# First two modulations as column-group products on TensorE in a two-layer hybrid decoder trunk: input asked for first, rotary tables spread late, planner numbers set anew

## Chip, cores and metric

The kernel runs on one core of one Trainium2 chip. The metric is the device time of one execution in microseconds (us), taken as the median over runs. A core has a matrix engine (TensorE, PE in the profile; PEld is its weight loading), VectorE (DVE), ScalarE (ACT), GpSimd (POOL) and SyncE (SP), which here only issues DMA transfers. Each engine works through its own queue in order.

## The reference

Everything is float32, with one sequence of 1024 rows of width 1024. Layer 0 mixes tokens by sparse attention (an indexer scores all keys, the 256 best are kept per query), layer 1 by a short gated convolution; each is followed by a SwiGLU network of width 2816.

```python
c_act = jax.nn.silu(c)
for i in range(2):
    mod = c_act @ ada_w[i] + ada_b[i]                   # (1, 1024) @ (1024, 6144)
    sh1, sc1, g1, sh2, sc2, g2 = jnp.split(mod, 6, -1)
    h = _rmsnorm(x, norm1_g[i]) * (1.0 + sc1) + sh1
    y = _dsa_mixer(h, ...) if i == 0 else _short_conv_mixer(h, ...)
    x = x + g1 * y
    h = _rmsnorm(x, norm2_g[i]) * (1.0 + sc2) + sh2
    x = x + g2 * _swiglu(h, w_gate[i], w_up[i], w_down[i])
```

Nothing of layer 0 can start before `sc1` and `sh1` of layer 0 (modulations j = 1 and j = 0 of the code) are there: each is a product of a vector of 1024 with a matrix of 1024 x 1024, 4 MB of weights.

## The kernel before

The program is recorded operation by operation (line 246 is the one line that issues them all) and put in order by a planner, class `Plan` (line 162). Every operation has a cost from `Plan.cost` (line 208), a priority `plan.pri` (a planned time in us, smaller first) and its dependencies; `drain` (line 394) plays the engines forward and always issues the operation that can start first, by priority among those that are ready. The numbers `LATENCY`, `SLACK`, `BIAS`, `CHANGE` and `STAY` (lines 164 to 171), the costs, and the planned times of `Attention` (`T_PROJ`, `SLOT`, `t_att`, `until`, lines 814 to 847) thus set the order of the whole program on each engine. The engines then run that order as it stands.

**Start, `first_norm` (line 857).** Eight row tiles of x, 128 x 1024 (512 KB), are loaded and transposed on TensorE; ScalarE squares each for the norm (`junk<-xs`), and ScalarE and VectorE each copy one half of each out of PSUM (`xt<-ps_mm`). `setup` (line 587) loads the small vectors, among them c, and makes `cact` = silu(c) in columns. `rope_tables` (line 727) computes sine and cosine rows, writes them to DRAM (`rd`) and reads them back four times each, spread over partitions into C and S; these ten transfers are issued on ScalarE's queue. The modulations j = 1 and then j = 0 are made from eight loads each of 128 x 1024 (512 KB). Of each load, columns 0 to 639 are multiplied and summed on VectorE (`ada_step`, `sc<-...,cact,sc`), with a sum over partitions on TensorE at the end (`ada_end`, `ps_sm<-ones,sc`); columns 640 to 1023 go through TensorE as three products whose moving operand is one column (`ada_pe`, `ps_mm<-cact,...`), each followed by an add on VectorE (`mod<-ps_mm,mod`). `ada_scale` turns j = 1 into `aff`. Then come, for each half of the 1024 tokens and each of 8 row blocks d, a product with `aff` and the norm on VectorE (`zs` for half 0, `nz` for half 1), the shift rounded to the matmul format on ScalarE (`hhi`) and its remainder on VectorE (`hlo`). x is spilled to DRAM (`xs<-xt`).

**Projections, `project` (line 926).** Each weight block is loaded (`raw`), rounded on ScalarE (`whi`), its remainder taken on VectorE (`wlo`), and used in three products per contraction block (hi hi, hi lo, lo hi). The order is: the index key (72 columns, below called the ki product), the index queries, K, Q in four groups j of 256 columns, V. Between them ScalarE and VectorE bisect for the 256th best score of each query, 31 rounds for each pair of blocks (`select`, line 1151; `junk<-sc,bs`), and `selected` (line 1194) turns the threshold into an additive mask (`bias`). Blocks (2, 3) and (6, 7) are counted on ScalarE, (4, 5) on VectorE; blocks 0 and 1 need no selection.

**Attention, `attend` (line 1217).** For each of 8 query blocks b and 4 key groups g: two paired products of 64 contraction rows (`ps_L<-karena,qst`), mask and maximum on VectorE (`p,mx<-ps_L,bias`), exp on ScalarE, transposes on TensorE (`ident,p`), copies (`pf`), and the products with V, which run as pairs into columns 0 to 63 and 64 to 127 of the array (`values`, line 1304, `ps_o<-pf,vst`, 128 x 64 weights each). `group_end` (line 1331) divides by the sums: reciprocals `rs`, widened by a copy to `rw` (128 x 256), two products of `rw` with the identity, and a multiplication. The gains and the second modulations of layer 0 are made by steps on VectorE in between (`ada_next`, line 1257).

After about 700 us the rest (both feed-forward networks, the convolution) is long chains of 128 x 512 products.

Of the kernel before, what the change touches and what calls it, by code (L numbers as in the profile page):

```python
# [161 lines left out]
class Plan:  # L162
# [3 lines left out]
    SLACK = (0.3, 0.1, 0.1, 0.1, 0.0)  # L166
    WINDOW = 3.41
    LANDING = 2.2
    BIAS = 0.8
    CHANGE = 0.097  # L170
    STAY = 4.0
# [36 lines left out]
    def cost(self, eng, fn, out, ins, kw):  # L208
# [7 lines left out]
        if eng == "tensor":  # L216
            if fn == "transpose":
                return 0.11, 0.0
            if ins[1].dtype in (F32R, BF16):
                return 0.0133 + n / 2400.0, 0.0  # L220
            return 0.112 if n < 64 else n * 4 / 2400.0, 0.0
# [3 lines left out]
        if eng == "scalar":  # L225
            if "accum_out" in kw:
                return 0.17 + 0.845e-3 * n + 0.1 * aps, 0.0
            return 0.04 + 0.83e-3 * n + (0.04 if out.dtype == F32R else 0.0), 0.0
        if eng == "vector":
            if fn == "memset":  # L230
                return 0.02 + 1.04e-3 * (n if n > P else 0), 0.0
            if fn in ("tensor_scalar", "tensor_copy") and not psum and "accum_out" not in kw:
                return (0.08 if fn == "tensor_copy" else 0.13) + 0.52e-3 * m, 0.0
            if fn == "tensor_scalar" and "accum_out" in kw:
                return 0.14 + 1.04e-3 * m, 0.0
            return 0.07 + 1.04e-3 * m + (0.05 * aps if m > 64 else 0.0), 0.0
# [216 lines left out]
P = 128  # L453
# [35 lines left out]
class Trunk:  # L489
# [97 lines left out]
    def setup(self, c, positions, ada_b, n1, n2, conv_w, gq, gk, lg, lb, rope_c, arenas, kgb):  # L587
# [11 lines left out]
        self.plan.pri = 1.2  # L599
# [47 lines left out]
    def ada_end(self, layer, j, lhs, half=0):  # L647
# [8 lines left out]
        dst = self.mod[layer][j]  # L656
        c0 = half * 4
# [3 lines left out]
        if j in (1, 4) and c0 + n == KT or layer == 0 and j == 1:  # L661
# [65 lines left out]
    def rope_tables(self, positions, C, S, tmp, dram):  # L727
# [18 lines left out]
        for i, (out, ph) in enumerate(((C, 0.25), (S, 0.0))):  # L746
# [9 lines left out]
            dr = dram.part_of(i)[i]  # L756
            nc.scalar.dma_start(dr.rearrange("c f t -> (c f) t"), n)
            for rep in range(4):
                nc.scalar.dma_start(
                    out.part_of(rep)[32 * rep:32 * rep + 32, :].rearrange("f (c t) -> f c t",  # L760
                                                                          c=4),
                    dr.rearrange("c f t -> f c t"))
# [50 lines left out]
class Attention:  # L813
    T_PROJ, SLOT = 45.0, 6.2
    ON_ACT, IDX = (2, 3, 6, 7), 0.5

    def __init__(self, tk, w, w_out, ada_w, xspill):
# [26 lines left out]
        cum = np.cumsum([0] + [6.8 * (b + 1) for b in range(TB)])  # L844
        w = np.array([0.0] * 5 + [41.0 / 26 * (c / 6.8 - 10) for c in cum[5:]])
        self.t_att = self.T_PROJ + 38 * self.SLOT + cum + w
        self.until = {2: self.t_att[2], 4: self.t_att[4] + 10.0, 6: self.t_att[7]}
# [9 lines left out]
    def first_norm(self, x, positions, setup):  # L857
# [1115 lines left out]
```

## Time and profile before

| | |
|---|---|
| median of 3 runs | 2283.16 us (2282.76 to 2283.68) |
| the profiled execution | 2284.37 us, of it 2282.7 us span |
| TensorE busy | 2237.3 us, 98% of the span |
| VectorE busy | 1820.4 us, 80% |
| ScalarE busy | 1131.4 us, 50% |
| DMA | 356.37 MB, 156 GB/s on average |

The profile shows one execution; times are counted from the start of the span. A busy TensorE is not one at its peak: the columns of the windows give the clock that was granted (1.00 is 2.4 GHz, 0.50 is 1.2 GHz). A product of float32 operands that are not rounded to the matmul format shows as two records.

### The profile page before, as it was taken

The numbers are of one execution on the slowest core, as the hardware profiler recorded it, in microseconds if no ns is written. First come the engines' busy times: TensorE is split into PE (matmuls) and PEld (weight loads), VectorE is DVE, ScalarE is ACT, GpSimd is POOL, SyncE is SP. The second block draws the span as 40 slices with busy tenths as digits, with TensorE's granted clock in tenths as the row PEclk, the third lists the DMA queues.
The fourth block names the chain that finished last, engine by engine and source line by source line (L and its number), as shares of the span: only waits on it lengthen the run. The fifth ranks groups of instructions, "written<-read, shape, count | busy, mean of one in ns | idle before, by whom it ended". The sixth has DMA issues, their size and how long they took to land.

```text
span 2282.7 us, 33002 instructions
## 1 busy us (share of the span) xinstructions
PE 2237.3 (98%) x11686; PEld 1820.7 (80%) x11686; DVE 1820.4 (80%) x3705; ACT 1131.4 (50%) x2148; POOL 4.1 (0%) x19
## 2 busy tenths in 40 slices
PE   7998999999999999999999999999999999999998
PEld 6666876777798888888888888788888888888887
DVE  5889999776579899987688899885798965667874
ACT  3577899856755333333344553244552333344443
POOL 0000000000000000000000000000000000000000
PEclk6999999999999999999999999999999999999999
DMA  8423233332234566765986154434345633348853
GB/s 273 157 74 84 82 120 91 107 94 66 88 113 138 174 209 203 234 212 183 311 303 213 52 148 134 124 94 165 106 149 175 204 113 99 119 152 308 300 176 97
DMA packets 334191, 356.37 MB, mean 156 GB/s; under 512 B 18089, under 2 KB 218826, under 8 KB 334026
## 3 DMA queue, kind: packets, MB, share of 16 engines
q1 hardware_dynamic: 332586, 352.96, 48.4%
q8 instruction: 91, 1.49, 0.3%
q10 hardware_dynamic: 1440, 1.31, 0.2%
q14 instruction: 74, 0.61, 0.1%
HBM read 282.64 MB, written 71.57 MB: 155 GB/s over the span
## 4 chain that ended last, share of the span: by engine, by line
PE 92%; DVE 4%; ACT 2%; DMA 1%; issue 1%; SPq 0%; ACTq 0%; DVEq 0%
PE ps_x L246 33%; PE ps_mm L246 28%; PE ps_z L246 18%; PE ps_sm L246 6%; PE ps_L L246 4%; PE ps_o L246 3%; ACT junk L246 1%; DVE u L246 0%; DMA raw<-in_conv_w_in_dram 0%; DVE p L246 0%; DMA xs<-in_x_dram 0%; DVE wlo L246 0%; DVE s L246 0%; ACT p L246 0%; DVE sc L246 0%
## 5 line engine op out<-in xcount | busy, mean ns | idle before, releaser
L246 ACT CAST whi<-s 128x512 fp32r<-128x512 f32 x311 | 192.7, 621 | 388.5 <-DVE s L246 116.0
L246 PE MATMUL ps_x<-t,whi 128*128 128x512 f32 x1016 | 314.4, 390 | 0.0
L246 ACT CAST whi<-raw 128x512 fp32r<-128x512 f32 (+1 forms) x228 | 139.5, 618 | 252.4 <-PE ps_z L246 84.4
L246 DVE TENSOR_TENSOR wlo<-s,whi 128x512 fp32r<-128x512 f32 x312 | 213.3, 688 | 47.5 <-ACT whi L246 46.3
L246 DVE TENSOR_TENSOR wlo<-raw,whi 128x512 fp32r<-128x512 f32 (+1 forms) x254 | 173.2, 686 | 75.2 <-ACT whi L246 74.4
L246 PEld LDWEIGHTS ps_x<-t,whi 128*128 128x128 f32 x1016 | 190.8, 188 | 39.6
L246 PE MATMUL ps_x<-t,wlo 128*128 128x512 f32 x508 | 198.1, 390 | 0.0
L246 PE MATMUL ps_x<-h,whi 128*128 128x512 f32 x536 | 165.6, 390 | 0.0
L246 PE MATMUL ps_z<-t,whi 128*128 128x512 f32 x488 | 150.9, 390 | 0.0
L246 DVE CUSTOM_DVE_ANT_0 p<-ps_L,bias 128x512 f32<-128x512 f32 (+3 forms) x192 | 100.3, 553 | 39.8 <-PE ps_L L246 16.7
L246 PE MATMUL ps_z<-h,whi 128*128 128x512 f32 x408 | 126.0, 390 | 0.0
L246 PE MATMUL ps_mm<-h,whi 128*128 128x512 f32 x400 | 123.3, 389 | 0.0
L246 PE MATMUL ps_x<-ph,whi 128*128 128x512 f32 x396 | 122.0, 389 | 0.0
L246 ACT ACTIVATE p<-p,nm,qsc 128x128 f32<-128x128 f32 (+7 forms) x128 | 111.4, 873 | 21.2 <-DVE nm L246 20.0
L246 ACT ACTIVATE junk<-sc,bs 128x896 bf16<-128x896 f32 (+3 forms) x124 | 109.4, 883 | 17.4 <-DVE bs L246 12.5
L246 PEld LDWEIGHTS ps_x<-h,whi 128*128 128x128 f32 x536 | 100.2, 188 | 20.5
L246 PEld LDWEIGHTS ps_x<-t,wlo 128*128 128x128 f32 x508 | 95.5, 188 | 20.2 <-DVE wlo L246 0.2
L246 PEld LDWEIGHTS ps_z<-t,whi 128*128 128x128 f32 x488 | 91.8, 188 | 19.4 <-ACT whi L246 0.3
L246 DVE TENSOR_TENSOR u<-u 128x512 f32<-128x512 f32 x152 | 103.5, 687 | 2.6 <-ACT u L246 0.8
L246 PE MATMUL ps_x<-h,wlo 128*128 128x512 f32 x268 | 104.6, 390 | 0.0
L246 PE MATMUL ps_mm<-hhi,wlo 128*128 128x512 f32 (+2 forms) x240 | 93.0, 389 | 7.3 <-DVE wlo L246 7.2
L246 PE MATMUL ps_z<-t,wlo 128*128 128x512 f32 x244 | 95.6, 392 | 3.9 <-DVE wlo L246 3.9
(379 smaller groups left out, 5406.6 us busy)
## 6 DMA issues: line engine op xcount, KB each, us to landing
adaw<-in_ada_w_dram SPq DMA_DIRECT2D x160, 256.0 KB
ph<-in_ffn_w_down_dram SPq DMA_DIRECT2D x66, 512.0 KB
raw<-in_ffn_w_gate_dram SPq DMA_DIRECT2D x54, 512.0 KB
raw<-in_ffn_w_up_dram SPq DMA_DIRECT2D x54, 512.0 KB
rt<-t SPq DMA_DIRECT2D x80, 256.0 KB
raw<-in_conv_w_in_dram SPq DMA_DIRECT2D x34, 512.0 KB
hid<-u SPq DMA_DIRECT2D x52, 256.0 KB
rt<-hid SPq DMA_DIRECT2D x48, 256.0 KB
```

What stands on the lines that cost most here:

```text
L246: f(*[a.get() if isinstance(a, Ref) else a for a in args], **{k: a.get() if isinstance(a, Ref) else a for k, a in kw.items()})
```

## The change

The first two modulations go to TensorE alone. `cpad` holds, for each of 8 contraction blocks, a 128 x 32 weight whose first column is `cact` and whose others are zero. Each modulation is loaded in two halves of 512 columns, eight loads of 128 x 512 (256 KB) for each half, all into staging tiles with no reuse. Four products of 128 x 32 weights with 128 x 512 float32 operands are issued together, each into its own 32 partitions of one PSUM bank; a second set of four is added on top. ScalarE or VectorE copies the 128 x 512 result, and four products with ones add up the partitions. The shift's modulation is tracked per half, so blocks d = 0 to 3 need only its first half.

```diff
-        bc = [tk.norm_bc(ss.part_of(half)[:, 4 * half:4 * half + 4], sp, "L")[:, 0:HW]
+        bc = [tk.norm_bc(ss.part_of(half)[:, 4 * half:4 * half + 4], sp, "mm")
               for half in range(NH)]
-        plan.pri = 1.5
-        tk.rope_tables(positions, self.C, self.S, self.score[4:2:-1], self.rd)
+        plan.pri = 9.5
+        spread = tk.rope_tables(positions, self.C, self.S, self.score[4:2:-1], self.rd)
+        plan.pri = 1.05
+        cpad = self.score[5][:, 0:32 * KT].rearrange("p (k m) -> p k m", m=32)
+        nc.vector.memset(cpad, 0.0)
+        nc.vector.tensor_copy(cpad[:, :, 0:1], tk.cact.unsqueeze(2))
         for j in (1, 0):
-            acc = self.score[5 + j][:, 0:5 * P]
-            pool, tag = (self.keep, "vst") if j else (self.hp, "lo0")
-            stage = pool.tile([P, 4, D], F32, name="stage%d" % j, tag=tag)
-            for k in range(KT):
-                plan.pri = 10.0 + k + 8 * (1 - j)
...
+            stage = [(self.keep if t == "vst" else self.hp).tile([P, 4, D], F32, name="stage", tag=t)
+                     for t in (("hi1", "vst") if j else ("hi0", "lo0"))]
+            acc, total = tk.ps("L"), self.s4()
+            for half in range(NH):
+                cs = half_of(half)
+                for k in range(KT):
+                    plan.pri = 10.0 + k + 8 * half + 16 * (1 - j)
+                    w = stage[k // 4].part_of((half, k))[:, k % 4, cs]
+                    last = nc.sync.dma_start(w, tk.ada_rows(self.ada_w, 0, j, k)[:, cs])
                 plan.pri = 1.1
-                tk.ada_step(w[:, 0:5 * P], k, acc)
-                tk.ada_pe(w[:, 5 * P:], 0, j, k, 5)
-            tk.ada_end(0, j, [acc])
+                ps = acc.part_of(half)[:, cs]
+                for k0 in (0, 4):
+                    plan.matmuls([(ps[32 * g:32 * g + 32], cpad[:, k0 + g],
+                                   stage[k0 // 4].part_of((half, k0 + g))[:, g, cs])
+                                  for g in range(4)], 1.667e-3, k0 == 0, k0 == 4, base=0.02)
+                row = total.part_of(half)[:, cs]
+                plan.copy(row, ps)
+                tk.ada_end(0, j, [row], half)
+        plan.pri, plan.gate = 42.5, last
+        spread()
+        plan.gate = None
...
-                tk.shift(z, tk.mod[0][0][:, d:d + 1], self.h[half](d))
+                tk.shift(z, tk.mod[0][0].part_of((0, 0, d // 4))[:, d:d + 1], self.h[half](d))
```

The norm's broadcast (`norm_bc`) moves from the PSUM ring `L` to the ring `mm`, which has two buffers and which the ki product uses too. The small loads of `setup` get priority 9.0 in place of 1.2, behind the eight loads of x. The rotary tables' transfers move from ScalarE's queue to SP's: each table is written when its sine is done, and the spreading reads wait for the last modulation load.

```diff
-            nc.scalar.dma_start(dr.rearrange("c f t -> (c f) t"), n)
...
+            nc.sync.dma_start(dram.part_of(i)[i].rearrange("c f t -> (c f) t"), n)
+
+        def spread():
+            for i, out in enumerate((C, S)):
+                for rep in range(4):
+                    nc.sync.dma_start(
...
```

In `group_end` the widening copy goes; four 64-column products take the reciprocals as a broadcast weight:

```diff
-        rw = sp.tile([P, GRP * HD], F32, name="rw", tag="rw")
-        plan.copy(rw.rearrange("p (r d) -> p r d", d=HD),
-                  rs.unsqueeze(2).to_broadcast([P, GRP, HD]))
         bc = self.bank()[:, 0:2 * P]
         for i in range(2):
-            nc.tensor.matmul(bc[:, blk(i)], rw[:, blk(i)], tk.ident, start=True, stop=True)
+            plan.matmuls([(bc[r * HD:(r + 1) * HD, blk(i)],
+                           rs[:, 2 * i + r:2 * i + r + 1].to_broadcast([P, HD]), tk.ident)
+                          for r in range(2)], 1.7e-3)
```

The planner's numbers and costs are set anew, of which two lines stand for all; `until`, which spreads the bisection rounds, ends later for the pairs (2, 3) and (6, 7), and eight modulation steps of attention move from block 2 to block 1.

```diff
-    SLACK = (0.3, 0.1, 0.1, 0.1, 0.0)
+    SLACK = (0.313, 0.045, 0.089, 0.1, 0.0)
...
-        self.until = {2: self.t_att[2], 4: self.t_att[4] + 10.0, 6: self.t_att[7]}
+        self.until = {2: self.t_att[2] + 17.951, 4: self.t_att[4] + 10, 6: self.t_att[7] + 32.655}
```

**What it moves.** SP's queue at the start (`xs` is x, `C`, `S` and `sc` receive the small vectors, `stage`, `raw` and `s` are weights, `rd` the tables in DRAM). Before, one tile of x stands in row 1, and then:

```order
9 L246 DMA S<-in_ada_b_dram 96x128
10 L246 DMA sc_239<-in_positions_dram 32x256 x2
11 L246 DMA S<-in_attn_k_norm_g_dram 1x64
12 L246 DMA sc_239<-in_positions_dram 32x256 x2
13 L246 DMA xs<-in_x_dram 128x1024 x7
14 L246 DMA raw<-in_ada_w_dram 128x1024
15 L246 DMA stage_233<-in_ada_w_dram 128x1024
16 L246 DMA s_247<-in_ada_w_dram 128x1024
```

Now all eight tiles of x stand in row 1, and behind the small vectors:

```order
11 L248 DMA S<-in_attn_k_norm_g_dram 1x64
12 L248 DMA sc_239<-in_positions_dram 32x256 x2
13 L248 DMA stage<-in_ada_w_dram 128x512 x16
14 L248 DMA rd<-sc_240 128x256
15 L248 DMA raw<-in_attn_w_in_dram 128x8x72
16 L248 DMA stage<-in_ada_w_dram 128x512 x12
17 L248 DMA rd<-sc_240 128x256
18 L248 DMA stage<-in_ada_w_dram 128x512 x4
19 L248 DMA raw<-in_attn_w_in_dram 128x4x256 x2
20 L248 DMA C<-rd 32x4x256 x4
21 L248 DMA S<-rd 32x4x256 x4
```

All of x thus stands ahead of the small vectors, the 16 loads of j = 1 follow these in one row, and two writes of tables, each of which waits for a sine on ScalarE, stand between the other modulation loads. Behind row 21 come the 16 spills of x and four weight loads.

TensorE from the modulations to the first product of the ki (`hhi`, `hlo` with `whi`, `wlo`). Before, the last rows of it:

```order
23 L246 MATMUL ps_mm<-cact,stage_407 128x1
24 L246 MATMUL ps_mm<-cact,raw 128x1 x3
25 L246 MATMUL ps_mm<-cact,stage_407 128x1 x2
26 L246 MATMUL ps_mm<-cact,s_249 128x1 x3
27 L246 MATMUL ps_mm<-cact,stage_407 128x1 x6
28 L246 MATMUL ps_mm<-cact,raw 128x1 x3
29 L246 MATMUL ps_mm<-cact,s_522 128x1 x3
30 L246 MATMUL ps_mm<-cact,stage_407 128x1 x3
31 L246 MATMUL ps_sm<-ones,sc_241 128x1 x5
32 L246 MATMUL ps_mm<-hhi_257,whi 72x512
```

Now, all of it:

```order
6 L248 MATMUL ps_L<-stage,sc_241 32x512 x4
7 L248 MATMUL ps_mm<-ident,xs 128x128 x3
8 L248 MATMUL ps_mm<-ident,nr 128x128 x5
9 L248 MATMUL ps_L<-stage,sc_241 32x512 x4
10 L248 MATMUL ps_mm<-ident,nr 128x128 x3
11 L248 MATMUL ps_sm<-ones,s_247 128x1 x4
12 L248 MATMUL ps_L<-stage,sc_241 32x512 x8
13 L248 MATMUL ps_sm<-ones,s_247 128x1 x4
14 L248 MATMUL ps_L<-stage,sc_241 32x512 x8
15 L248 MATMUL ps_sm<-ones,s_248 128x1 x4
16 L248 MATMUL ps_L<-stage,sc_241 32x512 x8
17 L248 MATMUL ps_mm<-hhi_591,whi 72x512
```

Eight sets of four products stand in place of 48 one-column ones, and the ki product starts ahead of the last four sums. Its 48 products were interleaved with the first index-query products; now its second half stands in one piece, behind all `nz` of VectorE.

VectorE between Q's groups j = 0 and j = 1 (`sw` and `rt` are the rotation of j = 0, `junk` and `bs` the bisection, `wlo` the weights of j = 1). Before:

```order
321 L246 TENSOR_TENSOR rt<-rt,C 128x512
322 L246 SCALAR_TENSOR_TENSOR bs<-bs 128x2
323 L246 TENSOR_TENSOR bs<-bs 128x2
324 L246 TENSOR_TENSOR rt<-rt,sw 128x512
325 L246 SCALAR_TENSOR_TENSOR bs<-bs 128x2
326 L246 TENSOR_SCALAR bs<-bs 128x2
327 L246 TENSOR_TENSOR bs<-bs 128x2
328 L246 TENSOR_SCALAR junk_245,bs<-sc_240,bs 128x640
329 L246 SCALAR_TENSOR_TENSOR bs<-bs 128x2
330 L246 TENSOR_SCALAR bs<-bs 128x2
331 L246 TENSOR_TENSOR wlo<-raw,whi 128x512
```

Now:

```order
277 L248 TENSOR_TENSOR sw<-rt,S 128x512
278 L248 TENSOR_SCALAR junk_245,bs<-sc_241,bs 128x768
279 L248 TENSOR_TENSOR rt<-rt,C 128x512
280 L248 TENSOR_TENSOR bs<-bs 128x2 x2
281 L248 TENSOR_TENSOR wlo<-raw,whi 128x512
282 L248 SCALAR_TENSOR_TENSOR bs<-bs 128x2 x2
283 L248 TENSOR_TENSOR sw<-rt,S 128x512
284 L248 TENSOR_SCALAR junk_245,bs<-sc_240,bs 128x640
285 L248 TENSOR_SCALAR bs<-bs 128x2
286 L248 TENSOR_TENSOR rt<-rt,sw 128x512
287 L248 TENSOR_SCALAR junk_245,bs<-sc_241,bs 128x768
```

The first `wlo` of j = 1 stood behind the whole rotation of j = 0 and five bisection passes that came in between; now it stands behind two of them and ahead of the last `sw` of that rotation. Further on, of the 192 masked products of attention on VectorE, 10 stood ahead of the mask of block 2, and now all 32 of blocks 0 and 1 do; the last bisection pass of blocks 4 and 5 moves from behind 46 masked products to behind 10. After the attention the order of all engines is nearly what it was.

## Rows read from the trace of the kernel before

**Rows 1.** The page: busy time of each engine, and the shares by engine of the chain that ended last.

```profile
PE 2237.3 (98%) x11686; PEld 1820.7 (80%) x11686; DVE 1820.4 (80%) x3705; ACT 1131.4 (50%) x2148; POOL 4.1 (0%) x19
PE 92%; DVE 4%; ACT 2%; DMA 1%; issue 1%; SPq 0%; ACTq 0%; DVEq 0%
```

**Rows 2.** Windows of the start: us, busy time of PE, PEld, DVE, ACT and POOL (with instructions), the granted clock, the DMA share and GB/s.

```profile
20.00:25.00 5.00, 4.92 (x23) 4.82 (x24) 3.69 (x10) 3.38 (x8) 0.00 (x0) 0.50 1.02 417
...
30.00:35.00 5.00, 5.00 (x25) 5.00 (x26) 3.64 (x8) 1.70 (x2) 0.00 (x0) 0.50 1.02 367
...
60.00:70.00 10.00, 9.48 (x30) 5.37 (x31) 9.76 (x15) 7.14 (x12) 0.00 (x0) 0.70 0.84 301
```

**Rows 3.** The timeline of the start: start us, us, engine, line, operation, out<-in, count, and the idle time before it with what ended it.

```profile
4.46 1.06 ACT L246 ACTIVATE junk<-xs 128x1024 bf16<-128x1024 f32 x1 [2.38 <-DMA xs<-in_x_dram]
...
7.40 3.50 SPq L246 DMA_DIRECT2D xs<-in_x_dram  x7
...
9.41 0.21 ACT L246 ACTIVATE cact<-vec 128x8 f32<-128x8 f32 x1 [1.82 <-DVE vec L246]
...
12.41 0.59 ACT L246 COPY xt<-ps_mm 128x512 f32<-128x512 f32 x1
...
12.89 1.06 ACT L246 ACTIVATE junk<-xs 128x1024 bf16<-128x1024 f32 x1
...
17.52 1.28 ACT L246 ACT_TABLE_LOAD   x1
...
20.08 0.80 PE L246 MATMUL ps_L<-ident,nr 128*128 128x128 f32 x2 [2.92 <-DVE nr L246]
...
20.43 1.06 ACT L246 ACTIVATE junk<-xs 128x1024 bf16<-128x1024 f32 x1
...
21.61 1.06 ACT L246 ACTIVATE junk<-xs 128x1024 bf16<-128x1024 f32 x1
...
38.43 0.99 PE L246 MATMUL ps_sm<-ones,sc 128*128 128x1 f32 x4
...
45.19 0.16 DVE L246 SCALAR_TENSOR_TENSOR aff<-mod,vec 128x8 f32<-128x8 f32 x1
```

**Rows 4.** The timeline from the last modulation loads' work to the index queries.

```profile
50.02 1.40 DVE L246 SCALAR_TENSOR_TENSOR zs<-xt,aff,ps_L 128x512 f32<-128x512 f32 x2
...
52.75 4.81 SPq L246 DMA_DIRECT2D xs<-xt  x7
...
59.99 0.70 PE L246 MATMUL ps_mm<-hhi,whi 128*72 128x512 f32 x1 [1.01 <-ACT hhi L246]
60.41 5.39 DVE L246 SCALAR_TENSOR_TENSOR hlo<-zs,mod,hhi 128x512 fp32r<-128x512 f32 x8
...
74.08 1.41 DVE L246 SCALAR_TENSOR_TENSOR hlo<-nz,mod,hhi 128x512 fp32r<-128x512 f32 x2
...
75.73 0.39 PE L246 MATMUL ps_mm<-hlo,whi 128*72 128x512 f32 x1
...
75.95 0.51 PE L246 MATMUL ps_mm<-hhi,wlo 128*72 128x512 f32 x2
...
88.28 0.38 PE L246 MATMUL ps_mm<-hhi,wlo 128*128 128x256 f32 x1 [0.71 <-DVE wlo L246]
```

**Rows 5.** DMA from 20 to 45 us in 40 slices: GB/s.

```profile
GB/s 395 426 420 419 420 419 420 419 420 336 313 241 220 252 246 342 328 324 334 393 406 367 383 403 408 419 418 419 413 387 288 200 169 200 297 305 370 324 279 225
```

**Rows 6.** TensorE's timeline at paired products: first the index scores (two of 64 rows at a time, 8 records are two pairs of 512 columns), then attention (`ps_o<-pf,vst`, pairs of 64 weight columns, 32 records are eight pairs of 128).

```profile
170.19 1.77 PE L246 MATMUL ps_L<-karena 64*128 64x512 f32 x8
171.90 0.50 PE L246 MATMUL ps_mm<-hhi,wlo 128*128 128x512 f32 x1
...
600.45 1.97 PE L246 MATMUL ps_o<-pf,vst 128*64 128x128 f32 x32
602.35 0.87 PE L246 MATMUL ps_mm<-ident,p 128*128 128x128 f32 x6
603.06 0.60 PE L246 MATMUL ps_sm<-ident,p 128*128 128x128 f32 x4
603.59 1.13 PE L246 MATMUL ps_L<-karena,qst 64*128 64x512 f32 x4
```

**Rows 7.** TensorE's and VectorE's timelines where Q's group j = 1 begins.

```profile
203.92 0.50 PE L246 MATMUL ps_mm<-hhi,whi 128*128 128x512 f32 x1 [1.14 <-ACT rt L246]
...
210.42 0.69 DVE L246 TENSOR_TENSOR wlo<-raw,whi 128x512 fp32r<-128x512 f32 x1
...
211.16 0.79 PE L246 MATMUL ps_mm<-hhi,wlo 128*128 128x512 f32 x1 [6.51 <-DVE wlo L246]
```

**Rows 8.** Windows there and where attention begins, columns as in rows 2.

```profile
210.00:215.00 5.00, 3.84 (x9) 3.06 (x10) 5.00 (x18) 3.29 (x7) 0.00 (x0) 0.50 1.01 235
...
315.00:320.00 5.00, 4.67 (x22) 2.67 (x22) 4.93 (x20) 4.99 (x19) 0.00 (x0) 0.51 0.16 52
320.00:325.00 5.00, 4.50 (x22) 2.90 (x20) 4.95 (x24) 5.00 (x21) 0.00 (x0) 0.50 0.32 104
```

**Rows 9.** The timelines at the start of attention: TensorE's first wait, and one of VectorE's steps for the mask of block 2, between the masked products of block 0.

```profile
313.58 0.91 PE L246 MATMUL ps_L<-karena,qst 64*128 64x128 f32 x8 [0.88 <-DVE mx L246]
...
315.30 0.96 DVE L246 TENSOR_TENSOR_SCAN s<-s 128x384 f32<-128x384 f32 x1
```

**Rows 10.** The operations on `rw` and what waited for them: count, shortest, median and longest ns, first and last start.

```profile
L246 ACT COPY rw<-rs x28: 387/405/440, 320.4 to 620.5; 128x256 f32<-128x256 f32 x28
```

More of the change, by code (lines that the diff above doesn't have):

```diff
@@ L227, in cost @@
                 return 0.17 + 0.845e-3 * n + 0.1 * aps, 0.0
-            return 0.04 + 0.83e-3 * n + (0.04 if out.dtype == F32R else 0.0), 0.0
+            return 0.045 + 0.84e-3 * n + (0.05 if out.dtype == F32R else 0.0) + 0.06 * aps, 0.0
         if eng == "vector":
@@ L232, in cost @@
             if fn in ("tensor_scalar", "tensor_copy") and not psum and "accum_out" not in kw:
[L233 removed]
+                return (0.13 if m > 64 and fn != "tensor_copy" else 0.08) + 0.52e-3 * m, 0.0
+            if fn == "tensor_tensor_scan":
+                return 0.07 + 2.09e-3 * m, 0.0
             if fn == "tensor_scalar" and "accum_out" in kw:
                 return 0.14 + 1.04e-3 * m, 0.0
[L236 removed]
+            return 0.07 + 1.04e-3 * m + (0.06 * aps if m > 64 else 0.0), 0.0
         if fn in ("memset", "affine_select"):
@@ L655, in ada_end @@
                 n += 1
-        dst = self.mod[layer][j]
-        c0 = half * 4
+        dst, c0 = self.mod[layer][j], half * 4
+        dst = dst if layer or j else dst.part_of((0, 0, half))
         b0 = layer * 48 + j * 8 + c0
@@ L660, in ada_end @@
                                 op=ALU.add)
-        if j in (1, 4) and c0 + n == KT or layer == 0 and j == 1:
+        if j in (1, 4) and c0 + n == KT:
             self.ada_scale(layer, j)
@@ L755, in rope_tables @@
             nc.scalar.activation(n, r, AF.Sin)
-            dr = dram.part_of(i)[i]
-            nc.scalar.dma_start(dr.rearrange("c f t -> (c f) t"), n)
[L758 to L762, printed above, removed]
+            nc.sync.dma_start(dram.part_of(i)[i].rearrange("c f t -> (c f) t"), n)
[3 more added lines that the diff above has]
+                    nc.sync.dma_start(
+                        out.part_of(rep)[32 * rep:32 * rep + 32, :].rearrange(
+                            "f (c t) -> f c t", c=4),
+                        dram.part_of(i)[i].rearrange("c f t -> f c t"))
+        return spread
     def rotate(self, ab, tmp, C, S):
@@ L843, in __init__ @@
         self.junk = [sel.tile([P, n], BF16, name="junk%d" % n) for n in (6 * P, T)]
-        cum = np.cumsum([0] + [6.8 * (b + 1) for b in range(TB)])
-        w = np.array([0.0] * 5 + [41.0 / 26 * (c / 6.8 - 10) for c in cum[5:]])
-        self.t_att = self.T_PROJ + 38 * self.SLOT + cum + w
-        self.until = {2: self.t_att[2], 4: self.t_att[4] + 10.0, 6: self.t_att[7]}
+        cum = np.cumsum([0] + [6.916 * (b + 1) for b in range(TB)])
+        w = np.array([0.0] * 5 + [1.317 * (c / 6.916 - 10) for c in cum[5:]])
+        self.t_att = self.T_PROJ + 37.582 * self.SLOT + cum + w
+        self.until = {2: self.t_att[2] + 17.951, 4: self.t_att[4] + 10, 6: self.t_att[7] + 32.655}
     def arena(self, i):
@@ L903, in first_norm @@
         for half in range(NH):
-            plan.pri = 27.0 + 4 * half
+            plan.pri = 43 + 4 * half
             hl = [self.hp.tile([P, KT, HW], F32R, name="h%s%d" % (v, half), tag="%s%d" % (v, half))
@@ L1231, in attend @@
             for g in range(KVH):
-                for _ in range((0, 0, 2, 2, 2, 2, 2, 2)[b]):
-                    plan.pri = t0 + (t1 - t0) * g / 4.0
+                for _ in range((0, 2, 0, 2, 2, 2, 2, 2)[b]):
+                    plan.pri = t0 + (t1 - t0) * g / 4.0 + -0.923
                     self.ada_next()
```

25 lines of the change are left out of this document (10 added, 15 removed).

## The prediction

> **What bounds the kernel now.** I read the page first: TensorE is busy 98% of the span and holds 92% of the chain that ended last [rows 1]. So time can come only from where TensorE idles, does little for its time, or runs at half clock. The windows show where that is. Until 60 us its granted clock is mostly 0.50, and it is "busy" with one-column products [rows 2]; the first product on the normed x, the ki product, starts at 59.99 and its last at 75.95 + 0.22 = 76.2 us [rows 4]. After that its two larger stalls are before 211 us and around 312 to 325 us [rows 7 to 9]. Whatever makes the ki product end sooner moves everything behind it by as much, if nothing behind it is late by itself.
>
> What sets 76.2? The timeline of the start: `cact` is ready at 9.41, but the second tile of x is only asked for at 7.40 [rows 3]; loads then run at up to 426 GB/s until past 40 us [rows 5]; `aff` is ready at 45.19 [rows 3]; and from there VectorE has 32 steps of about 0.70 us (0.70 for a `zs`, 5.39 / 8 = 0.67 for a `hlo`) [rows 4], plus the remains of the second modulation, until the last `hlo` ends at 74.08 + 1.41 = 75.5 [rows 4]. So data first, then one-column products, then VectorE.
>
> **Term 1, the start: 14 us gained (ends 5 and 20).** x first: the first tile is squared at 4.46 [rows 3]; seven more of 512 KB at 420 GB/s [rows 5] take 7 x 1.25 = 8.7 us, so x is in by about 13.5. ScalarE is slower than that. A square takes a slot of 21.61 - 20.43 = 1.18, a copy one of 12.89 - 12.41 = 0.48, a table load 1.28 [rows 3]. The new order puts eight squares, seven copies, two table loads and two roots ahead of `cact`: 9.4 + 3.4 + 2.6 + 0.4 = 15.8, so `cact` comes at 4.5 + 15.8 = 20.3, 11 us later than now, and the first set of products at 21. Of the 16 loads of j = 1 (4.2 MB, 10 us) the last lands near 24.5. SP stops at the first table write until the sine, about 22; the 16 loads in the queue cover most of that. The second write waits for a sine that ScalarE does behind the copies of j = 1, near 31; the 12 loads ahead of it (3.1 MB, 7.5 us) keep the queues full until about 32, and the last four land at 36 to 38. The table reads and x's spills, 24 issues of about 4.81 / 7 = 0.69 us [rows 4], stand ahead of the weights of the second index query; they end near 54, and those weights are wanted at 70: hidden.
>
> A set of four products: one pair in two row halves takes, for 512 columns, (171.90 - 170.19) / 2 = 0.85 us, and a pair in two column halves (602.35 - 600.45) / 8 = 0.24 for 128 columns [rows 6], while one float32 product of 128 columns alone is 0.40 at half clock (two in 0.80 at 20.08) [rows 3], so two in turn would be 0.40 at full clock. Two column groups thus run side by side. Four at once the trace doesn't show. Bounds: four as dear as two pairs in turn, 1.71 us at full clock, or as one pair, 0.85. I take 0.85, since each of the four, like each of a pair, has its own columns; at half clock 1.71. The clock is the other unknown. The nearest rows, dense transposes at 20 to 25 us, have 0.50 [rows 2], so I take half clock.
>
> `aff` then needs 21 + 4 sets x 1.71 + 8 norm broadcasts x 0.40 [rows 3] + copy, four sums (0.99 [rows 3]) and add, 2.4 = 33.5 to 34. VectorE's 32 steps, a `wlo` and three small adds, 23.5 us, end at 57.5; the sums of j = 0 arrive before their `hlo` does. The second half of the ki product now holds the PSUM buffer of a norm broadcast, so it waits for the last `nz`, 2.8 us before that end, and then needs 24 x 0.22 = 5.3 [rows 4] at full clock, about 2 more at its start at half: 62. Before, eight products of the next kind (about 0.9 us) were done by 76.2. Gain 76.2 - 62 - 0.9 = 13.3, and 0.7 for the wait at 88.28 [rows 4], as the weights now come in time: 14. Full clock gives about 20. Sets at twice the price, at half clock, put 6.8 us more ahead of `aff`: 7, and some 2 more if ScalarE is late: 5.
>
> The Trainium skill (TensorE: Matmul & The Clock Gate, Part 3: Packing small matmuls) measured 3.07 times for four row tiles. No row here shows four; by it a set would cost 4 x 0.85 / 3.07 = 1.11 us at full clock (an estimate), and term 1 would be 2 us smaller.
>
> **Term 2, Q's group j = 1: 4 gained (ends -4 and 10).** TensorE waits 1.14 + 6.51 us there and then runs at 0.50 [rows 7, 8]; its 14 products at twice the time cost some 3 more. The `wlo` starts at 210.42 [rows 7]; VectorE had the rotation of j = 0 and five bisection passes ahead of it. In the new order the first `wlo` has two of the passes ahead and not the last `sw`, about half of that work, but the third, needed 12 products (2.7 us) later, still has the last rotation ahead. I let half of the stall go. What is late next is that third `wlo`. Lower end: a similar stall elsewhere in the new order.
>
> **Term 3, the start of attention: 3 gained (ends -3 and 6).** VectorE makes block 2's mask (a scan of 0.96 us among it) between block 0's masked products; TensorE waits for them, 0.88 the first time [rows 9], and runs at 0.51 and 0.50 for 10 us [rows 8]. The new order does this behind all 32 masked products of blocks 0 and 1. Most of the 6 us (2 idle, up to 4 of clock) could go. But the eight modulation steps now come into block 1.
>
> **Term 4, switches of array shape: 1.4 lost (0 to 3).** `group_end` now has four 64-column products, two pairs of 0.24, for two of 128 columns: even. But the order has 255 changes of shape in attention, for 240. A change's price: four transposes take 0.53 to the next, paired product, where six take 0.71, or 0.12 each, to the next transpose [rows 6]: 0.05 to 0.1 us. 15 x 0.09 = 1.4.
>
> The Trainium skill (TensorEngine Tiling (Array Packing), Tiling Modes) says that a change of tiling mode drains TensorE, which speaks against this edit and against sets between transposes. By the rows the drain is under 0.1 us, so it decides nothing.
>
> **Term 5, the copy `rw`: 0.5 gained (0 to 2).** 28 copies of 0.405 [rows 10] leave ScalarE, 11 us; while TensorE has other products this is hidden, and if that cover went it would be worth at most those waits on `rw`, about 0.5 each.
>
> Sum: 14 + 4 + 3 - 1.4 + 0.5 = 20.1 from the profiled execution's 2284.4: 2264.3. That execution is 1.2 above the median, so **2263 us**.
>
> **The rivals.**
> *The four products do not run side by side.* For: no row shows four. Against: pairs do [rows 6]. In turn, at half clock, 32 x 1.71 = 55 us and the sums put j = 0's second half at about 82, eight `hlo` follow (5.6) and the ki product ends near 89, 13 later than now; with terms 2 to 5 (+6) that is about 2290, slower. It decides from about 6 us a set; at full clock, or two at a time, it is not slower, about 2272.
>
> *The gain is spent behind the start.* The mask of block 2, now behind 32 masked products, comes too late: its steps take some 5 us, TensorE falls to half clock for as long again, and term 2 stays: 2263 + 10 + 4 = 2277. For: VectorE and ScalarE are nearly full there, 4.93 and 4.99 of 5 us [rows 8]. Against: the bisection of blocks 4 and 5 then is done.
>
> *Both stalls go and the clock is up early*: 2263 less 6 each for terms 1 and 2 and 3 for term 3, their ends, is 2248. For: the stalls are matters of order alone. Against: the half clock at the start is not.
>
> *The change doesn't do what it says*: x is first, but ScalarE, not the loads, sets `cact`; with waits between its steps at 25 instead of 20 it costs 4: 2267, inside the forecast.
>
> **How the numbers follow.** Forecast (2254 to 2271) 0.57; both stalls gone 0.15; gain spent, or two at a time (2271 to 2279) 0.14; about no change 0.06; in turn at half clock, or a worse order, 0.08. A measurement of this kernel tells 0.2% (4.6 us) from no change, so faster means under 2278.6: 0.57 + 0.15 + 0.14 = 0.86; same 0.06; slower 0.08. The range 2246 to 2277 leaves out 0.04 below and 0.16 above.
>
> **What would show it.** Right: `cact` near 20, `aff` near 34, the ki product's end near 62; a set of four in 0.85 or 1.71 us by the clock; the stall before Q's group j = 1 about half, no masked product of block 0 waiting for a scan. Wrong: a set of over 3 us; `aff` after 45; a new stall of over 5 us between 180 and 450 us; or a stretch after 700 us that differs, since there the order is nearly the same.

## The result and the profile after

The changed kernel takes 2267.86 us (median of 4 runs, 2267.19 to 2269.05) against 2282.96 before (4 runs): a ratio of 0.9937, 95% interval 0.9924 to 0.9949, 15.1 us less. The forecast was 2263. The profiled execution took 2268.15, its span is 2266.0; against the one of before that is 16.2, and 16.7 by the spans.

The page, answering to [rows 1]: nothing moved between the engines, TensorE has fewer idle and slow microseconds.

```profile
PE 2229.8 (98%) x11794; PEld 1800.1 (79%) x11794; DVE 1805.7 (80%) x3671; ACT 1122.1 (50%) x2125; POOL 5.3 (0%) x19
PE 92%; DVE 4%; DMA 2%; ACT 1%; issue 1%; SPq 0%; ACTq 0%; DVEq 0%
```

Where the gain stands is read by setting the start of the same record in both traces side by side:

| record | before | after | sooner by |
|---|---|---|---|
| first ki product | 59.99 | 45.76 | 14.2 |
| 145th `ps_mm<-hhi,whi` of the projections (ahead of Q's j = 1) | 200.06 | 186.60 | 13.5 |
| 151st of these (Q, j = 1) | 216.53 | 196.00 | 20.5 |
| last of these | 286.40 | 272.97 | 13.4 |
| first product of queries and keys in attention (`ps_L<-karena,qst`) | 311.99 | 298.56 | 13.4 |
| 33rd of these (the first of block 1) | 324.10 | 311.21 | 12.9 |
| first `ps_mm<-ohi,whi` (output projection, done while blocks 4 and 5 run) | 419.36 | 407.84 | 11.5 |
| 67th of these | 519.46 | 501.12 | 18.3 |
| first product of the feed-forward network | 672.66 | 655.81 | 16.8 |
| last transpose of the program | 2277.43 | 2260.84 | 16.6 |

So: the start gives 13 to 14, Q wins 7 and loses it again, attention first loses 2 (0.5 of it in block 0) and then wins 5, the rest is level.

**The start.** Windows of after, columns as in [rows 2]: from about 20.7 us on the clock is 1.00, not 0.50.

```profile
20.00:25.00 5.00, 3.67 (x26) 2.15 (x25) 3.52 (x11) 2.55 (x4) 0.00 (x0) 1.00 0.89 290
...
30.00:35.00 5.00, 3.75 (x20) 1.05 (x12) 2.17 (x7) 1.25 (x3) 0.00 (x0) 1.00 1.09 365
...
60.00:70.00 10.00, 9.04 (x77) 8.07 (x76) 5.06 (x13) 3.13 (x6) 0.00 (x0) 1.00 0.53 170
```

Ahead of that the windows print 1.00 too, but the record of the clock in this execution begins only at 20.7 us. The transposes tell what it was: eight of them take 1.97 us at 15.04 and 1.10 at 21.38, so TensorE was at half the clock until about 20.5.

```profile
15.04 1.97 PE L248 MATMUL ps_mm<-ident,xs 128*128 128x128 f32 x8 [2.10 <-DVE xt L248]
...
21.38 1.10 PE L248 MATMUL ps_mm<-ident,xs 128*128 128x128 f32 x8 [0.52 <-ACT xt L248]
```

The timeline of after, answering to [rows 3, 4]: `cact`, one set of four products (8 records) and the transposes behind it, two later sets, `aff`, the ki product's first, the first of its second half and its end (61.6, where the next kind begins).

```profile
22.64 0.21 ACT L248 ACTIVATE cact<-vec 128x8 f32<-128x8 f32 x1
...
23.64 1.06 PE L248 MATMUL ps_L<-stage,sc 128*32 128x512 f32 x8
24.63 0.55 PE L248 MATMUL ps_mm<-ident,xs 128*128 128x128 f32 x3
...
35.56 4.53 PE L248 MATMUL ps_L<-stage,sc 128*32 128x512 f32 x16
...
35.99 0.17 DVE L248 SCALAR_TENSOR_TENSOR aff<-mod,vec 128x8 f32<-128x8 f32 x1
...
45.76 0.46 PE L248 MATMUL ps_mm<-hhi,whi 128*72 128x512 f32 x1
...
55.96 0.46 PE L248 MATMUL ps_mm<-hhi,whi 128*72 128x512 f32 x1 [1.76 <-ACT s L248]
...
61.58 0.28 PE L248 MATMUL ps_mm<-hhi,whi 128*128 128x256 f32 x1
```

The first set leaves TensorE after 24.63 - 23.64 = 0.99 us, but the two sets at 35.56 take 4.53: most products behind the third set start one by one, as their loads land.

SP's queue: the first seven small loads behind x's eight tiles take 8.9 us to ask for, 1.3 each, and the other seven 0.4 each (before, all 14 took 6.1), so the modulation loads begin only at 16.82; the windows of DMA (share, GB/s at their end) show the hole.

```profile
0.80 4.04 SPq L248 DMA_DIRECT2D xs<-in_x_dram  x8
...
9.90 0.22 SPq L248 DMA_DIRECT2D C<-in_rope_c_dram  x1
11.18 0.22 SPq L248 DMA_DIRECT2D S<-in_attn_q_norm_g_dram  x1
...
16.82 9.91 SPq L248 DMA_DIRECT2D stage<-in_ada_w_dram  x16
```

```profile
15.00:20.00 5.00, 4.17 (x18) 3.55 (x19) 2.24 (x10) 3.35 (x7) 0.00 (x0) 1.00 0.54 160
```

**Q.** The wait for `wlo` [rows 7] is gone, and others stand in its place. SP asks for K (`karena<-kd`) and then for weights; ScalarE comes to the cast of these weights at 205.9 and stands 5.64 us until they land, with the bisection passes and `qsq` queued behind it; TensorE then waits for `qsq`, and its clock falls.

```profile
187.68 0.66 SPq L248 DMA_DIRECT2D karena<-kd  x1
...
194.46 5.24 SPq L248 DMA_DIRECT2D raw<-in_attn_w_in_dram  x2
```

```profile
189.30 0.50 PE L248 MATMUL ps_mm<-hhi,whi 128*128 128x512 f32 x1 [1.99 <-ACT qsq L248]
...
211.50 0.62 ACT L248 CAST whi<-raw 128x512 fp32r<-128x512 f32 x1 [5.64 <-DMA raw<-in_attn_w_in_dram]
...
217.13 0.39 PE L248 MATMUL ps_sm<-blk,qsq 128*128 128x4 f32 x2 [1.24 <-ACT qsq L248]
...
221.99 3.11 PE L248 MATMUL ps_sm<-blk,qsq 128*128 128x4 f32 x14 [2.08 <-ACT qsq L248]
```

```profile
220.00:225.00 5.00, 3.01 (x15) 3.01 (x15) 4.34 (x13) 4.94 (x11) 0.00 (x0) 0.71 0.40 109
225.00:230.00 5.00, 5.00 (x15) 3.98 (x16) 4.24 (x18) 2.02 (x6) 0.00 (x0) 0.61 0.51 142
```

**Attention.** Answering to [rows 8, 9]: no scan is between the masked products any more, but TensorE waits 2.93 us where it waited 2.16, and the clock falls for 10.2 us as before. ScalarE's table load, behind which the first exponential comes, stood there before too, and so did modulation steps on VectorE; a weight's remainder has come in. TensorE's waits before, from 311 to 322 us (total, times, longest), and ScalarE's table load:

```profile
PE ps_L L246 <- DVE mx L246: 1.3, 2, 0.9
PE ps_mm L246 <- ACT rw L246: 0.5, 1, 0.5
PE ps_mm L246 <- ACT p L246: 0.3, 1, 0.3
```

```profile
314.56 1.28 ACT L246 ACT_TABLE_LOAD   x1
```

After:

```profile
300.13 0.91 PE L248 MATMUL ps_L<-karena,qst 64*128 64x128 f32 x8 [0.86 <-DVE mx L248]
...
301.51 1.28 ACT L248 ACT_TABLE_LOAD   x1
...
301.78 0.49 PE L248 MATMUL ps_L<-karena,qst 64*128 64x128 f32 x4 [0.73 <-DVE mx L248]
...
303.44 0.33 PE L248 MATMUL ps_mm<-ident,p 128*128 128x128 f32 x1 [1.17 <-ACT p L248]
...
304.44 0.95 PE L248 MATMUL ps_mm<-ident,p 128*128 128x128 f32 x2 [0.17 <-ACT p L248]
```

What it wins later is idle time. TensorE's waits from 380 to 530 us (total, times, longest), before and then after:

```profile
PE ps_L L246 <- DVE mx L246: 3.5, 3, 1.4
PE ps_mm L246 <- ACT pf L246: 1.2, 1, 1.2
PE ps_sm L246 <- DVE pf L246: 0.6, 1, 0.6
PE ps_mm L246 <- DVE pf L246: 0.3, 1, 0.3
```

```profile
PE ps_L L248 <- DVE mx L248: 1.9, 3, 0.8
PE ps_sm L248 <- DVE pf L248: 0.3, 1, 0.3
```

### The profile page after: what moved, and what is told of

Read it like the earlier page. It is cut to its first block, busy times and chain, and to the rows that moved or that the text cites. A ratio compares the mean times of both kernels' runs of the same rounds, so it can differ in the third digit from the quotient of the medians.

```text
span 2266.0 us, 33149 instructions
## 1 busy us (share of the span) xinstructions
PE 2229.8 (98%) x11794; PEld 1800.1 (79%) x11794; DVE 1805.7 (80%) x3671; ACT 1122.1 (50%) x2125; POOL 5.3 (0%) x19
## 4 chain that ended last, share of the span: by engine, by line
PE 92%; DVE 4%; DMA 2%; ACT 1%; issue 1%; SPq 0%; ACTq 0%; DVEq 0%
PE ps_x L248 34%; PE ps_mm L248 25%; PE ps_z L248 18%; PE ps_sm L248 6%; PE ps_L L248 5%; PE ps_o L248 3%; DMA raw<-in_attn_w_in_dram 1%; DVE junk L248 1%; ACT junk L248 0%; SPq L248 0%; DMA xs<-in_x_dram 0%; DVE wlo L248 0%; DVE bs L248 0%; DVE rt L248 0%; DVE hlo L248 0%
## 5 line engine op out<-in xcount | busy, mean ns | idle before, releaser
L248 ACT ACTIVATE p<-p,nm,qsc 128x256 f32<-128x256 f32 (+7 forms) x128 | 111.3, 872 | 22.3 <-DVE nm L248 17.0
L248 PEld LDWEIGHTS ps_x<-h,whi 128*128 128x128 f32 x536 | 100.1, 188 | 20.5
L248 PE MATMUL ps_mm<-hhi,whi 128*128 128x512 f32 (+2 forms) x240 | 93.9, 391 | 4.2 <-ACT qsq L248 2.0
```

Source lines behind the costliest of these rows:

```text
L248: f(*[a.get() if isinstance(a, Ref) else a for a in args], **{k: a.get() if isinstance(a, Ref) else a for k, a in kw.items()})
```

## The experiments

Each is the changed kernel with one edit unless it says otherwise; their medians are to be set against 2267.86 for the change, and their ratios are to the kernel before, measured with each at 2282.4 to 2282.9.

**Which part carries the gain.** `old_numbers` puts every number of the planner back, `numbers_alone` puts the new numbers into the kernel before.

> The changed kernel with every number of the planner as before (SLACK, BIAS, CHANGE, STAY, the costs, T_PROJ, IDX, t_att, until, the offsets, the eight modulation steps in block 2); the new start and the four 64-column products of group_end stay. Theory: the gain of 15 is made at the start (the ki product ends 14 us sooner) and the numbers bring about nothing net: they take the stall ahead of Q's group j = 1 away (6 us), bring a new one of as much, and gain some 3 in attention. Then this kernel keeps the ki product near 62, has the old stall of about 6.5 us near 197, and takes 2268 to 2272. Rival: the numbers are what keeps the start's gain alive behind it; without them it is spent, and this takes 2276 or more.

> The kernel before with the planner's numbers of the change alone; start, table transfers and group_end as before. Theory (the gain is the start's): 2278 to 2284, the ki product's end at 76 as before; what it gains lies behind 400 us, where the changed kernel gained 5 us on the one before. Rival (the numbers carry it): 2272 or less.

Measured: 2275.02 (ratio 0.9972, 0.9962 to 0.9983) and 2282.24 (0.9998, 0.999 to 1.0007). With old numbers the ki product ends at 62.1 and the stall before Q's j = 1 is back with 6.0 us, as its theory had it; attention begins 11.8 sooner than before, and 10.2 remain at the end. Its time lies between theory and rival. `numbers_alone` came out within its theory's range. Its profiled execution shows that the numbers do move things on the old start (the ki product ends at 72.6, attention begins 8.6 sooner), but only 4.8 are left at the end of that execution, and by the medians nothing that can be told. So the start alone gives 8 by the medians, the numbers alone about 0, and both together 15: the numbers are worth 7, on the new start only.

**Are the sets of four what makes it fast?**

```diff
-                for k0 in (0, 4):
-                    plan.matmuls([(ps[32 * g:32 * g + 32], cpad[:, k0 + g], ...) for g in range(4)], ...
+                for k in range(KT):
+                    plan.matmuls([(ps[0:32], cpad[:, k], ...)], 1.667e-3, k == 0, k == KT - 1, base=0.02)
```

> The changed kernel with the products of the first two modulations in turn: all eight of a half accumulate in the same 32 partitions, so no two can run side by side. Theory: side by side matters. 32 products of about 0.85 us at the full clock are 27 us, against 8.4 MB of loads that take 20 to 25; TensorE, which holds the 0 to 60 us stretch's clock at 1.00, becomes the bound from 24 us on, aff comes at 39 to 41 in place of 36, the last sums at 54 to 56 in place of 47.5, and the ki product ends at 66 to 68: 2272 to 2275. Rival: the loads alone set the pace of the start, and the products hide behind them either way: aff at 36 to 37 and 2268 within 1.5. Second rival: half clock comes back, and it takes 2283 or more.

Measured: 2293.08 (1.0047, 1.0033 to 1.006), a time that only the second rival allows, though the products ran at the full clock: 32 records are 16 products in 13.92 us, 0.87 each. (Copies and sums run over 32 partitions in place of 128. The modulations that this kernel makes are not the reference's, and why stays open; every load and product is there.)

```profile
31.54 13.92 PE L248 MATMUL ps_L<-stage,sc 128*32 128x512 f32 x32 [0.66 <-ACT s L248]
...
37.77 0.57 ACT L248 COPY s<-ps_L 32x512 f32<-32x512 f32 x1 [3.02 <-PE ps_L L248]
...
54.56 1.05 PE L248 MATMUL ps_sm<-ones,s 32*128 32x1 f32 x8
```

The same copy, of j = 1's second half, in after:

```profile
33.95 0.58 ACT L248 COPY s<-ps_L 128x512 f32<-128x512 f32 x1
```

Four in turn are 3.48; the set of four frees TensorE after 0.99, 3.5 times sooner. The Trainium skill (TensorE: Matmul & The Clock Gate, Part 3: Packing small matmuls) has 3.07 for four row tiles, by which a set would be 1.13 (an estimate); these column groups did a little better. The time of this run does not price the products: the planner, whose rule `STAY` holds on to a shape, put all sums behind all products, at 54.56, so `aff` came at 57.23. The copies do: in turn, that of j = 1's second half comes 3.8 us later. With the sums right behind it `aff` would have come near 40 (an estimate, 36.0 + 3.8), as the theory had it; the other 17 us are the order. So `aff` owes some 4 us to the products running side by side.

**Q's new wait.** `k_late` records K's load behind the weights of j = 2. Only eight rows of SP move.

```diff
-        self.load_k()
         for j in range(HEADS // 4):
             w = tk.wpair(self.w, j * 2 * P)
+            if j == 2:
+                plan.gate = tk.loaded   # the load issued last
+                self.load_k()
+                plan.gate = None
```

> The changed kernel with the two loads of K into karena (1 MB each) asked for behind the weight loads of Q's group j = 2 instead of ahead of them; every other engine's order is the same, row by row. Theory: TensorE's two waits for qsq (1.24 us at 217 and 2.08 at 222, and the half clock behind them) come from ScalarE, which stood 5.64 us at a cast whose weights were late behind those two loads. Then that wait is under 1 us, both of TensorE's are gone, the clock stays at 1.00 there, and the kernel takes 2260 to 2263. Rival: the bisection passes ahead of qsq on ScalarE make it late, not the loads; then TensorE waits as before and it takes 2267 to 2268.

Measured: 2263.72 (0.992, 0.9908 to 0.9933), 4.1 under the change; no other run of this study is faster beyond doubt. Both waits for `qsq` behind 215 us are gone, and windows of `k_late` show TensorE full at the full clock there:

```profile
215.00:220.00 5.00, 5.00 (x24) 4.17 (x24) 4.67 (x17) 4.67 (x12) 0.00 (x0) 1.00 0.53 141
220.00:225.00 5.00, 5.00 (x30) 4.40 (x30) 4.88 (x19) 3.70 (x10) 0.00 (x0) 1.00 0.58 134
```

All of the difference is made there: 4.3 sooner at the end of Q, 4.4 at the end of the program. The theory held. The wait of 1.99 at 189.30 stayed (190.19 here): it stands behind a bisection pass and a cast on ScalarE, ahead of K's load.

**The start's hole in the DMA.** Two ways to bring the modulation loads forward, `vectors_on_act` and `vectors_first`.

> The changed kernel with the small loads out of the way of the modulations: c, the norm weights, the convolution's weights, the rotary frequencies and the two q and k gains (7 loads, on which cact hangs) are issued on ScalarE's queue before its first square, and the other 7 (index norm, ada_b, positions) on SP behind the first eight modulation loads. Theory: aff at 36 was set by data, since SP spent 4.96 to 16.82 on small loads behind x, about 1.3 us for one, while the DMA engines fell to 160 GB/s. Then the modulation loads follow x at once, the last of j = 1 lands 8 to 10 us sooner, cact is ready near 12, aff comes at 26 to 29, the ki product ends at 52 to 56 instead of 61.6, and 5 to 8 us of it last to the end: 2260 to 2263. Rival: ScalarE's squares and copies and the norm broadcasts set the start; then aff or the first norm step comes no sooner than 33 and it takes 2266 or more.

> The changed kernel with the small loads asked for ahead of x's tiles 2 to 8 again, as before (priority 1.2 in place of 9.0), and nothing else. Theory of the queue: in an empty queue SP issues a small load in about 0.4 us (1.28 to 7.40 in the kernel before), behind x in 1.3; so asking for x first costs the modulations more than it gives x: their loads start near 11 instead of 16.8, cact is ready near 12 instead of 22.6, aff comes at 31 to 33, and it takes 2263 to 2266. Rival: x first is worth what it looks like (x lands 6 us sooner and ScalarE's squares with it); then aff comes no sooner and the norm's broadcasts later, and it takes 2270 or more.

Measured: 2273.25 (0.9961, 0.9949 to 0.9973) and 2273.94 (0.9967, 0.9957 to 0.9977; 12 runs, 2270.18 to 2282.60): both slower than the change, and within the times of their rivals. In `vectors_on_act` the modulation loads began at 7.86 and the sums of j = 1 were done at 33.3, 2.3 sooner, but `mod` stood on VectorE behind the sine's table, which waits for the first table write, in SP's queue behind the loads:

```profile
35.08 0.62 DVE L248 TENSOR_SCALAR sc<-sc 128x256 f32<-128x256 f32 x2 [1.16 <-DMA rd<-sc]
...
36.08 0.15 DVE L248 TENSOR_TENSOR mod<-ps_sm,adab 128x4 f32<-128x4 f32 x1
```

`aff` came at 36.54, and at 34.67 in `vectors_first`. So in the first this wait held `aff` back, and not the squares and broadcasts of its rival; in the second the loads were asked for only from 13.83 on, not near 11. The times don't tell what the start is worth, since the order behind it changed too: against the change, attention began 2.8 and 0.2 sooner and ended 6.6 and 6.5 later. `vectors_first` also shows a set of four at half the clock (0.60 in that window), which leaves TensorE after 1.82:

```profile
22.31 1.88 PE L248 MATMUL ps_L<-stage,sc 128*32 128x512 f32 x8
24.13 0.66 PE L248 MATMUL ps_mm<-ident,xs 128*128 128x128 f32 x4
```

**Terms 4 and 5, and the start of attention:** `rw_back` and `exp_early`.

> The changed kernel with group_end as before: 28 or so copies rw back on ScalarE or VectorE, two 128-column products instead of four 64-column ones. Theory (terms 4 and 5 of the forecast): 1.4 lost by the changes of shape and 0.5 gained by the copy nearly cancel, so it takes 2266 to 2269. Rival: the copy was worth more than its busy time, because TensorE stood before the products of rw in block 0 and the clock fell with it; then it takes 2270 to 2274. The order of all attention moves a little with this edit, which alone may be worth 1 to 2 us either way.

> The changed kernel with one exponential of 128 x 1 more, on ScalarE right behind the norms of Q, so that the table load of 1.28 us that stood at 301.51, between the first masked products and their exponentials, falls into V's products. Theory: block 0 starts late because ScalarE's bisection pass (1.15) and table load (1.28) come before the first exponential; without the load the first transposes come 1.3 us sooner, the wait of 1.17 there goes, and it takes 2265 to 2267, or 2262 if the half clock of the 10 us behind goes too. Rival: VectorE (masked products, modulation steps, a bisection pass) sets the pace there, and TensorE's waits only change their releaser: 2267 to 2269.

Measured: 2274.92 (0.9969, 0.9958 to 0.998) and 2272.28 (0.9956, 0.9944 to 0.9968). Both are slower than any of their theories allowed, and neither settles its term, since the order of attention changed with them: `rw_back` was 2.2 sooner than the change at the first product of queries and keys and 6.2 later at the last. The profiled execution of `exp_early` is its slowest (2276.78, the fastest 2269.09); it was 5.9 late already before Q's j = 1, where its order is still that of the change, for the reason told at the end. In the row of `group_end` its own price is seen: the four 64-column products free TensorE after 0.59 (561.41 to 562.00), the two wide ones before after 0.54 (553.50 to 554.04); 0.05 x 32 = 1.6.

`k_late_exp` is `k_late` with the exponential, and every row of the order held:

```diff
+            if b == 4:   # V's copy of block 4, then one exponential of qsn into ssq
+                op.emit = lambda: (first(), second())
```

> k_late with the exponential of 128 x 1 placed behind the copy of V's fifth block on ScalarE, every engine's order otherwise held row by row (the run exp_early had let the planner make a new order, which cost 9 us elsewhere before attention even began). Theory: the table load of 1.28 us then falls into V's products and the first transposes of block 0 come 1.2 us sooner; the wait of 1.18 for p goes and it takes 2260 to 2262.5. Rival: VectorE sets the pace of block 0, and it takes 2263 to 2264.

Measured: 2263.52 (0.992, 0.9906 to 0.9933): the rival. The wait for `p` went, and the one for VectorE grew from 0.84 to 2.30, because the table load delayed a cast `whi` on ScalarE, and with it the `wlo` that stands ahead of the masked products on VectorE (294.22 in `k_late`, 295.73 here):

```profile
297.30 0.92 PE L248 MATMUL ps_L<-karena,qst 64*128 64x128 f32 x8 [2.30 <-DVE mx L248]
```

> k_late_exp with 7 of the 14 small loads (c, norm, convolution and gain vectors) issued on ScalarE's queue before its first square, all other rows of every engine held in order. Theory: SP spends 1.3 us on each small load behind x, so the modulation loads start 4 to 6 us sooner, aff comes at 31 to 33 instead of 36, the ki product ends 3 to 4 us sooner and, as the order behind is the same, nearly all of it lasts: 3 us faster than k_late_exp. Rival: another member of the start is as late as the loads (cact behind ScalarE's squares, the norm broadcasts behind x's transposes, VectorE's 32 steps): less than 1 us faster, or slower by the 2.7 us that ScalarE spends on the issues.

Measured: 2266.84 (0.9934, 0.9922 to 0.9946): slower. SP's eight requests for x took 8.56 us beside the second queue (4.04 in after), the modulation loads began at 17.25 and `aff` came at 36.20: the theory fell. Taking small loads away from SP did not shorten its wait. In `vectors_on_act` four modulation loads behind x are asked for 1.28 us apart as well (11.50 to 15.35), and 1.28 us is about what x's tile of 512 KB takes at 410 GB/s (an estimate from [rows 5]). So SP seems to wait for room behind x, whatever it asks for; that was not tested by itself. Nor are the 3.3 us all the start's: the ki product ended 1.1 later than in `k_late_exp`, and behind it the clock of the profiled execution fell to 0.50, where `k_late_exp` kept 1.00.

**Is the order itself worth something?** `k_late` with no edit but one of the planner's numbers moved by a twentieth.

```diff
-    CHANGE = 0.082
+    CHANGE = 0.086
```

> k_late with one number of the planner moved by a twentieth: CHANGE 0.086 in place of 0.082. Nothing else; the order differs from row 652 of TensorE on, in attention, and the start and the projections are the same row by row. Theory: the kernels with another order in attention (rw_back, exp_early, both runs with moved vectors) all lost 6 to 9 us between 390 and 520 us, whatever their edit was for, because the numbers were set for one order and hold for it alone. Then this one loses too, without any edit: 2267 to 2272. Rival: those losses belong to their edits, and a neighbouring order is as good: 2262 to 2265.

> k_late with another number moved by a twentieth: the cost of a scan, 2.2 in place of 2.09 ns a column. The order differs in blocks 2 to 7 of attention alone. Theory (the set order is worth several us by itself): 2266 to 2272. Rival (a neighbouring order is as good): 2262 to 2265.

Measured: 2273.80 (0.9962, 0.9950 to 0.9974) and 2270.53 (0.9949, 0.9936 to 0.9963): 10.1 and 6.8 slower than `k_late`, all of it in attention. TensorE's longest waits of `p_change` from 380 to 530 us, to be set beside those of after above, which `k_late` has too:

```profile
PE ps_L L248 <- DVE mx L248: 3.8, 6, 0.8
PE ps_mm L248 <- ACT pf L248: 1.9, 2, 1.4
PE ps_mm L248 <- ACT p L248: 1.4, 1, 1.4
PE ps_mm L248 <- DVE x L248: 0.5, 1, 0.5
```

So the losses of `rw_back`, `vectors_on_act` and `vectors_first` in attention need no cause in their edits: each of the two neighbouring orders tried costs as much. `exp_early`, which the expectation counts among them, does not belong there: it was 8.2 later than the change at the first output projection and 8.4 at the 67th.

## Why the prediction was right, and where it was not

**Term 1 (14): right in size, by errors that cancel.** The ki product ended at 61.6, forecast 62, and attention began 13.4 sooner. The clock was 1.00 from 20.7 us on where half was taken, by the forecast's own working worth some 6. Against that `cact` came at 22.64 instead of 20.3, and the loads of j = 1 were asked for from 16.82 on: the forecast priced them by bandwidth right behind x, and not the small loads between. By its own sum the full clock would have put `aff` near 21 + 3.4 + 1.6 + 2.4 = 28.4; the loads kept it at 35.99, 2 behind the forecast. A set took 0.99 where 0.85 was taken for this clock and 1.82 where 1.71 was taken for the other. (The 0.40 for a single float32 product is a misreading without harm: the two records in 0.80 at 20.08 are one product, and at 22.45 such records follow 0.21 apart, 0.43 a product.) The second half of the ki product began at 55.96 and needed 5.6; forecast was 54.7 and 5.3.

**Term 2 (4): 0.** The stall before j = 1 went as a whole, 7 sooner there, but waits of another kind took all 7 back by 230 us. The forecast looked for what is late next on VectorE, its third `wlo`; it was a weight load behind K's loads, and it passed through ScalarE's queue. `k_late` shows it: with K's load behind those weights 4.1 of these come back.

**Term 3 (3): -0.5 in block 0, -2 by the output projection.** The step that failed is that the work on block 2's mask sets TensorE's pace in block 0. With the scan gone TensorE waited 0.8 longer and the half clock lasted as long. The forecast left out ScalarE's table load of 1.28 us, which stood ahead of the first exponential before and after; and `k_late_exp` shows that with that piece taken away VectorE's wait grows instead. The other 1.5, in blocks 1 to 3, were not traced to a cause.

**Terms 4 and 5 (-1.4 and 0.5).** The products of `group_end` cost 1.6 by their rows; the whole was not measured alone. The Trainium skill (TensorEngine Tiling (Array Packing), Tiling Modes) has a change of mode drain TensorE. The trace leaves little for it: the transposes follow a set 0.99 after its start, where one product alone takes 0.87, so at most 0.12, and in `group_end` 0.05 for four products in place of two.

**What no term held: some 5 while blocks 4 and 5 run.** It comes from the set order: between the same two records, the first of the output projection and the first of the feed-forward network, `p_change` loses 0.6 on before and `p_scan` wins 2.0. With terms 2 and 3 as measured the forecast would have been 2263 + 4 + 5 = 2272; this brought it to 2268. That the sum came within 5 us of the measurement is thus luck in part, in term 1 and in the whole.

**The rivals.** The sets run side by side, so the slow rival fell; but its price for products in turn at the full clock, about 2272, left out what the planner would do with them (`in_turn`, 2293.08). "Gain spent behind the start" was wrong of the start, whose 13.4 reached attention, and right that term 2 would come to nothing, though by new waits and not by the old one or the mask. ScalarE's `cact` was late by 2.3 of the 5 that rival gave it.

## What to carry to other kernels

Before costing a load by bandwidth, read the queue that issues it: what stands between it and the transfer ahead, and which in-order engine will come to its consumer first. Where a planner's numbers were fitted to one program, the gain of an edit and the gain of its order cannot be told apart by undoing the edit; hold the order row by row, or run a kernel with no edit and a moved number, as a measure of what the order alone is worth (here 7 and 10 us in two tries, half the change and more).

## What the runs showed that I had not expected

From 20.7 us on TensorE stayed at 1.00 through the start of after, with waits up to 1.76 us among transposes and sets of 512 columns, while before it stood at 0.50 though recorded as busy nearly all the time, among transposes and one-column products [rows 2]. Which of these made the difference was not tried. One thin place may decide several us from execution to execution: the transposes behind the ki product. In the change they waited 0.96 us and the clock stayed at 1.00; in the profiled execution of `exp_early`, with the same order up to there, they waited 2.98, and the clock fell. That, and not a new order as the expectation of `k_late_exp` has it, made it late before attention, by 5.8 and not by 9. The length of this wait alone does not decide: the clock fell behind 1.13 in `vectors_on_act` too, and not behind 1.96 in `old_numbers`.

```profile
69.83 0.47 PE L248 MATMUL ps_o<-ident,s 72*128 72x72 f32 x4 [2.98 <-DVE sc L248]
```

```profile
70.00:75.00 5.00, 5.00 (x37) 4.80 (x37) 4.76 (x11) 0.79 (x2) 0.00 (x0) 0.64 0.30 76
```
